# Hybrid encoder trunk on one core: first FFN's weight loads cut into halves and quarters, two adaLN sums moved to the stage's head, last FFN's adaLN loads issued ahead of its units

## The chip, the cores and the metric

The kernel runs on one core of one Trainium2 chip. The time is what the device takes for one execution, in microseconds (us); shown are the median of three runs and one further execution that the hardware profiler recorded. Differences here are a per cent or less, so every argument is about single stalls in the recorded execution.

## The reference

A trunk of two layers on a sequence of 512 tokens, width 1024, all in float32. Layer 0 mixes tokens with a gated short convolution, layer 1 with a Mamba-2 scan; each is followed by a SwiGLU feed-forward block (FFN) of width 2816. Every sub-layer is normed before and after, and shifted, scaled and gated by vectors that come from one conditioning vector `c`:

```python
mod = (jax.nn.silu(c) @ ada_w + ada_b).reshape(bsz, DEPTH, 2, 3, D_MODEL)
for i in range(DEPTH):
    shift, scale, gate = (mod[:, i, 0, k][:, None, :] for k in range(3))
    h = rmsnorm(x, norm_g[i, 0]) * (1.0 + scale) + shift
    y = short_conv_mixer(...) if i % N_MIXERS == 0 else ssd_mixer(...)
    x = x + gate * rmsnorm(y, norm_g[i, 1])
    shift, scale, gate = (mod[:, i, 1, k][:, None, :] for k in range(3))
    h = rmsnorm(x, norm_g[i, 2]) * (1.0 + scale) + shift
    y = swiglu_ffn(h, f_w_in[i], f_w_out[i])      # (silu(gate) * up) @ w_out
    x = x + gate * rmsnorm(y, norm_g[i, 3])
```

`silu(c) @ ada_w` is a vector times a 1024 x 12288 matrix: 48 MB of weights that are read once and used for almost no arithmetic. The kernel spreads these sums ("adaLN sums") over the whole program.

## The kernel before

**Arithmetic.** A float32 matrix product is made of three reduced-precision ones: each operand is split into a high part (a cast by ACT, lines 230 and 616) and a low part (the difference, by DVE, lines 231 and 617), and PE multiplies high by high, high by low and low by high. So every weight tile passes through one ACT and one DVE instruction after its load and before its matmuls.

**adaLN sums.** One sum (`ada_madd`, lines 125 and 127) multiplies 128 rows by 1024 columns of `ada_w` (a 512 KB load into a tile `ada_st`) by a column of `silu(c)` and adds it to an accumulator on DVE. Eight sums make one vector; then `ada_fold` (line 140) reduces the accumulator, `ada_fin` (line 147) finishes it with one small matmul, and four small additions write it. In the first FFN, `ada_steps` owns three `ada_st` buffers: as soon as a sum has read its buffer, `ada_load` (line 1004) issues the load for the sum three further on. `sums(n)` does the next n sums; 48 are done in this stage. In the last FFN, `gate_late` does eight sums for the very last gate vector, with two buffers that lie in a tile `raw`, which is not yet in use there.

**The first FFN** (it is the code around line 1345). At its head, PE finishes the last products of six column tiles that were begun before (`rest`), while DVE and ACT prepare other forms of the activations (`Values`). Then come six units (class `Units`), in which a 2 x 2 block product is done with seven products instead of eight; each unit fetches its weights in five loads (`fetch`, lines 602 to 608), and two further DMAs of GpSimd's queue (`add_`, line 1228) add weight blocks in place. Line 605 writes into the buffer that the last such addition has read, so it waits for that addition to land. After the units comes a loop over plain column tiles, k = 18 to 37. One tile is 24 matmuls of 128 x 512 (`in_chunk`). Per tile the loop also issues:

- every second tile, one load of 1 MB for the pair of tiles k + 4 and k + 5 (`load_pair_at`, through line 221, tile `wst`);
- at k = 18, 22 and 26 one load of 1 MB of the FFN's second weight matrix (`x_load`, line 1234, tile `w2x`);
- the splits of the weights of tile k + 2 (lines 230 and 231);
- two adaLN sums, with three at k = 24, and with each sum one load of 512 KB.

**The last FFN** has the same head and then 16 units. In unit u it calls `next(late, None)` behind `c12`, which is one step of `gate_late`: the first step issues the loads 0, 1 and, behind the first sum, 2; the eighth step does the last sum and the fold.

**Order.** In both FFNs the order on SP (which issues nearly all loads), ACT, DVE and GpSimd is the order of the code, and PE's is so throughout. An instruction that waits holds back all that stands behind it on its engine. On SP this means that a load that waits for a buffer holds back all later loads.

Of the kernel before, what the change touches and what calls it, by code (L numbers as in the profile page):

```python
# [8 lines left out]
F32 = mybir.dt.float32  # L9
F32R = mybir.dt.float32r  # L10
# [6 lines left out]
P = 128  # L17
T = 512
D = 1024
KD = D // P  # L20
DFF = 2816
# [17 lines left out]
def trunk_kernel(  # L39
# [175 lines left out]
    def load_w(srcs, nk=KD, k0=0, later=None):  # L215


        st = wst_p.tile([P, 8, 256], F32, tag="wst", name="wst")
        o = 0
        for m, c0, n in srcs:  # L220
            dma(st[:, :nk, o:o + n], m[k0 * P:(k0 + nk) * P, c0:c0 + n].rearrange("(k p) f -> p k f", p=P))
            o += n
        res = []
        for b in range(o // P):
            w = whl_p.tile([P, 2, 8, P], F32R, tag="whl", name="whl")
            sw = st[:, :nk, b * P:(b + 1) * P]
            if later is None:
                split_w(sw, w, nk)
            else:
                later.append((lambda sw=sw, w=w: act.copy(w[:, 0, :nk, :], sw),  # L230
                              lambda sw=sw, w=w: dve.tensor_tensor(w[:, 1, :nk, :], sw,  # L231
                                                                   w[:, 0, :nk, :].bitcast(F32), SUB)))
            res.append(w)
        return res
# [517 lines left out]
    with ExitStack() as ph:  # L752
# [477 lines left out]
        def w_rows(p, c, n=1):  # L1230
            return w2[2 * p * P:2 * (p + n) * P, c * T:(c + 1) * T].rearrange("(k p) f -> p k f", p=P)

        def x_load(u):
            dma(wx[u].rearrange("p i r f -> p (i r) f"), w_rows(2 * u, 0, 2))

        def y_load(p):
            wy[p] = hp.tile([P, 2, T], F32, tag=f"h{p}", name="w2y")
# [96 lines left out]
        with tc.manual_schedule(engines={PE_ENGINE, mybir.EngineType.SP, mybir.EngineType.Activation,  # L1334
# [11 lines left out]
                vs.value(j)  # L1346
            vs.first()
            vs.hi(0, va[:, :, lo_])
            rest(2)
            vs.value(4)  # L1350
            vs.value(5)
# [113 lines left out]
            splits = {k0 + i: op for i, op in enumerate(splits[5:])}  # L1465
            todo_w, todo_s = [], []

            def load_pair_at(k):
                got = []
                new = load_w([(f_w_in[0], (k - 2) // 2 % 2 * DFF + (4 + (k - 2) // 4 * 2) * P, 256)], later=got)  # L1470
                for i in range(2):
                    ws[k + i], splits[k + i] = new[i], got[i]

            for k in range(k0, last + 1):
                if k % 2 == 0 and k + 4 <= last:
                    load_pair_at(k + 4)
                if k in (k0, k0 + 4, k0 + 8):
                    x_load((k - k0) // 4)
                if k in (last - 2, last - 1):
                    xy_load(n_s - 2 + k - last + 2)  # L1480
                tiles[k] = in_chunk(ws[k], h)
                for step in todo:
                    next(step, None)
                q, j = divmod(k - 3, 4)
                if j < 2:
                    gate(4 + 2 * q + j, tiles[k - 1])
                else:
                    up(2 + 2 * q + j, tiles[k - 1])
                for op in splits.get(k + 2, ()):
                    op()  # L1490
                low_parts()
                sums(3 if k == k0 + 6 else 2)
                if k == 2 * NF - 12:
                    ggs.append(make_gg(1, gg_tile))
                if k == last - 1:
                    assert next(madds, 0) == 0 and not ada_sets and not quarters
                    sums_p.close()
                    ph.enter_context(tc.tile_pool(name="gap", bufs=1, side="right", reuse_waits="tile")).tile(
                        [P, 216], F32, tag="gap", name="gap")
                    ao_p.append(ph.enter_context(tc.tile_pool(name="aop", bufs=3, side="right", reuse_waits="tile")))  # L1500
                    ao_p[0].tile([P, 2, 2, 256], F32R, tag="ao", name="ao")
                    gotp = ph.enter_context(tc.tile_pool(name="gotp", bufs=1, side="right", reuse_waits="tile"))
                    c22 = gotp.tile([P, 2, T], F32, tag="c22", name="c22")
                if k >= last - 1:
                    w_prep(seq[k - last + 1])
                    a_prep(seq[k - last + 1])
# [563 lines left out]
    with ExitStack() as ph:  # L2070
# [137 lines left out]
        with tc.manual_schedule(engines={PE_ENGINE, mybir.EngineType.SP, mybir.EngineType.Activation,  # L2208
# [22 lines left out]
            def gate_late():  # L2231

                st = [raw[:, 18 + 2 * b:20 + 2 * b, :].rearrange("p a b -> p (a b)") for b in range(2)]
                acc = s1t[:, 7:11, :].rearrange("p a b -> p (a b)")
                part = s1t[:, 6, P:P + 32]

                def load(k):
                    if k < KD:
                        dma(st[k % 2], ada_w[k * P:(k + 1) * P, 88 * P:96 * P])

                load(0)
                load(1)
                for k in range(KD):
                    ada_madd(acc, st[k % 2], k)
                    load(k + 2)
                    if k == KD - 1:
                        ada_fold(acc, part)
                    yield
                yield from ada_fin(88 * P, part)
                yield from put_gates(3)  # L2250

# [39 lines left out]
            up(2, acc)  # L2291
            t_four(0)
            late = gate_late()
            for u in range(UN):
                v = u - 1
                last = u == UN - 1
                if u + 2 <= UN:
                    fetch(u + 2)
                elif last:
                    tail = []  # L2300
                    n12 = load_w([(w1, 21 * P, P), (w1, DFF + 20 * P, P)], later=tail)
                product(u, "P1")
                if u:
                    c12(v)
                    next(late, None)
                else:
                    t_four(1)
                    up(3, acc2)
                split_x(u + 1)
                if u:  # L2310
                    product(v, "P7")
                keep(u, "A", 0, LO)
                product(u, "P5")
                if u:
                    c22(v)
                    s13()
                product(u, "P2")
                keep(u, "C", 1, HI)
                if u:
                    product(v, "P4")  # L2320
                c11(u)
                split_z(u)
                if not last:
                    sum_y(u + 1)
                    sum_s(u + 1)
                product(u, "P6")
                if u:
                    c21(v)
                if last:
                    for op in tail[0]:  # L2330
                        op()
                    n3 = load_w([(w1, DFF + 21 * P, P)], later=tail)
                else:
                    split_y(u + 1)
                product(u, "P3")
                keep(u, "A", 0, HI)
                if not last:
                    split_s(u + 1)
# [184 lines left out]
```

## Time and profile before

| | us |
|---|---|
| median of three runs | 1345.19 (1344.96 to 1347.11) |
| the profiled execution, whole | 1347.34 |
| its span, first to last instruction | 1345.6 |
| PE busy in the span | 1314.5 |
| DVE busy | 1049.8 |
| ACT busy | 662.6 |

PE idles for 31 us in all. The rows that the next parts show are of these kinds. In a list of instructions by time, a row gives start and duration in us, engine, source line, operation, what it writes and reads, how many were merged, and in brackets how long the engine was idle ahead of it and whose end released it. In a table of stretches, the columns are the stretch, its length, then busy time of PE, PE's weight loads, DVE, ACT and GpSimd (POOL) with their number of instructions, then the granted PE clock as a share of full speed, the share of the time that the 16 DMA engines were busy, and GB/s. SPq is the queue of SP. "DMA a<-b" is a transfer in flight.

### The profile page before, as it was taken

The numbers are of one execution on the slowest core, as the hardware profiler recorded it, in microseconds if no ns is written. First come the engines' busy times: TensorE is split into PE (matmuls) and PEld (weight loads), VectorE is DVE, ScalarE is ACT, GpSimd is POOL, SyncE is SP. The second block draws the span as 40 slices with busy tenths as digits, with TensorE's granted clock in tenths as the row PEclk, the third lists the DMA queues.
The fourth block names the chain that finished last, engine by engine and source line by source line (L and its number), as shares of the span: only waits on it lengthen the run. The fifth ranks groups of instructions, "written<-read, shape, count | busy, mean of one in ns | idle before, by whom it ended". The sixth has DMA issues, their size and how long they took to land.

```text
span 1345.6 us, 19807 instructions
## 1 busy us (share of the span) xinstructions
PE 1314.5 (98%) x7653; PEld 1143.0 (85%) x7653; DVE 1049.8 (78%) x1627; ACT 662.6 (49%) x1084; POOL 99.5 (7%) x123
## 2 busy tenths in 40 slices
PE   8999999999999999999999999999999799999998
PEld 6788889998877788898888888888899799998886
DVE  5578667887877886768998988987678687776888
ACT  5333355443122565655555455564474354554665
POOL 0000000110000140000000000000002112100330
PEclk9999999999999999999999999999999899999999
DMA  9767742587888892415444334323334699768871
GB/s 311 235 205 242 236 153 60 152 209 233 291 311 278 231 177 71 121 33 162 139 118 133 104 100 131 121 79 120 131 87 110 189 248 236 196 165 285 186 140 63
DMA packets 209698, 228.53 MB, mean 170 GB/s; under 512 B 9396, under 2 KB 163908, under 8 KB 208580
## 3 DMA queue, kind: packets, MB, share of 16 engines
q1 hardware_dynamic: 191008, 187.88, 44.9%
q0 software_dynamic: 14448, 26.48, 11.4%
q10 hardware_dynamic: 4148, 12.90, 2.9%
q8 instruction: 60, 0.98, 0.3%
q14 instruction: 34, 0.28, 0.1%
HBM read 198.52 MB, written 2.24 MB: 149 GB/s over the span
## 4 chain that ended last, share of the span: by engine, by line
PE 82%; DMA 8%; DVE 5%; SPq 2%; ACT 2%; issue 2%; DVEq 0%; ACTq 0%; POOLq 0%
PE ip L285 10%; PE ip L287 10%; PE ip L286 10%; PE y L387 10%; PE sA L654 8%; DMA ada_st<-in_ada_w_dram 5%; PE cA L2205 4%; PE sC L654 4%; PE cA L1309 3%; PE li L285 2%; PE li L287 2%; PE li L286 2%; PE sB L654 2%; DVE ada_acc L127 2%; PE li L936 1%
## 5 line engine op out<-in xcount | busy, mean ns | idle before, releaser
L287 PE MATMUL ip<-h,whl 128*128 128x512 f32 x744 | 290.7, 391 | 5.6 <-DVE whl L231 5.6
L285 PE MATMUL ip<-h,whl 128*128 128x512 f32 x744 | 294.0, 395 | 1.8 <-ACT whl L230 1.6
L286 PE MATMUL ip<-h,whl 128*128 128x512 f32 x744 | 289.8, 389 | 0.0
L287 PEld LDWEIGHTS ip<-h,whl 128*128 128x128 f32 x744 | 139.7, 188 | 37.9 <-DVE whl L231 8.5
L285 PEld LDWEIGHTS ip<-h,whl 128*128 128x128 f32 x744 | 139.8, 188 | 31.5 <-ACT whl L230 1.8
L286 PEld LDWEIGHTS ip<-h,whl 128*128 128x128 f32 x744 | 139.8, 188 | 28.0
L231 DVE TENSOR_TENSOR whl<-wst,whl 128x1024 fp32r<-128x1024 f32 x86 | 104.4, 1219 | 31.3 <-ACT whl L230 31.3
L654 PE MATMUL sA<-tq,whl 128*128 128x256 f32 x792 | 106.0, 289 | 11.7 <-DVE g L681 9.8
L230 ACT CAST whl<-wst 128x1024 fp32r<-128x1024 f32 x86 | 89.2, 1042 | 48.6 <-DMA wst<-in_f_w_in_dram 46.4
L654 PEld LDWEIGHTS sA<-tq,whl 128*128 128x128 f32 x792 | 101.2, 197 | 13.2 <-DVE g L681 10.4
L127 DVE SCALAR_TENSOR_TENSOR ada_acc<-ada_st,csil,ada_acc 128x1024 f32<-128x1024 f32 x63 | 80.7, 1281 | 19.6 <-DMA ada_st<-in_ada_w_dram 19.1
L387 PE MATMUL y<-whlo,ys 128*128 128x512 f32 x384 | 89.4, 392 | 0.0
L387 PEld LDWEIGHTS y<-whlo,ys 128*128 128x128 f32 x384 | 71.7, 188 | 15.9 <-issue 0.6
L285 PE MATMUL li<-h,whl 128*128 128x256 f32 x288 | 83.2, 289 | 0.0
L287 PE MATMUL li<-h,whl 128*128 128x256 f32 x288 | 81.6, 283 | 0.0
L286 PE MATMUL li<-h,whl 128*128 128x256 f32 x288 | 81.5, 283 | 0.0
L617 DVE TENSOR_TENSOR whl<-wsu,whl 128x1024 fp32r<-128x1024 f32 x46 | 56.2, 1222 | 25.0 <-ACT whl L616 25.0
L1668 DVE SCALAR_TENSOR_TENSOR cu<-ip,cols,cu 128x511 f32<-128x511 f32 (+2 forms) x84 | 62.8, 748 | 3.9 <-ACT cu L1665 1.4
L2205 PE MATMUL cA<-whlo,ao 128*128 128x512 f32 x264 | 61.0, 390 | 0.4 <-DVE c L2436 0.2
L2205 PEld LDWEIGHTS cA<-whlo,ao 128*128 128x128 f32 x264 | 49.3, 188 | 11.5 <-ACT whlo L2170 1.2
L285 PEld LDWEIGHTS li<-h,whl 128*128 128x128 f32 x288 | 55.3, 192 | 0.0
L1228 POOL DMA_DIRECT2D sg<-sg x22 | 19.1, 870 | 488.5 <-DMA sg<-in_f_w_in_dram 287.9
(383 smaller groups left out, 2527.8 us busy)
## 6 DMA issues: line engine op xcount, KB each, us to landing
ada_st<-in_ada_w_dram SPq DMA_DIRECT2D x88, 512.0 KB, 6.0
wst<-in_f_w_in_dram SPq DMA_DIRECT2D x18, 1024.0 KB, 6.1
wst<-in_m_w_in_dram SPq DMA_DIRECT2D x14, 1024.0 KB, 5.3
wsu<-in_f_w_in_dram SPq DMA_DIRECT2D x24, 512.0 KB, 5.7
sg<-in_f_w_in_dram SPq DMA_DIRECT2D x44, 256.0 KB, 3.3
wsu<-in_f_w_in_dram SPq DMA_DIRECT2D x44, 256.0 KB, 3.9
wst<-in_m_w_in_dram SPq DMA_DIRECT2D x20, 512.0 KB, 4.8
wst<-in_a_w_in_dram SPq DMA_DIRECT2D x9, 1024.0 KB, 7.8
```

What stands on the lines that cost most here:

```text
L127: dve.scalar_tensor_tensor(acc, w, csil[:, k:k + 1], acc, MUL, ADD)
L230: later.append((lambda sw=sw, w=w: act.copy(w[:, 0, :nk, :], sw), lambda sw=sw, w=w: dve.tensor_tensor(w[:, 1, :nk, :], sw, w[:, 0, :nk, : ...
L231: lambda sw=sw, w=w: dve.tensor_tensor(w[:, 1, :nk, :], sw, w[:, 0, :nk, :].bitcast(F32), SUB)))
L285: pe.matmul(dst, w_at(w, 0, kk), a[:, 0, sl], start=start, stop=False)
L286: pe.matmul(dst, w_at(w, 0, kk), a[:, 1, sl], start=False, stop=False)
L287: pe.matmul(dst, w_at(w, 1, kk), a[:, 0, sl], start=False, stop=stop)
L387: pe.matmul(pst, a[:, al, tk], wt[:, wl, kk, :], start=k == 0 and i == 0, stop=k == K - 1 and i == 2, skip_group_check=bool(held))
L617: dve.tensor_tensor(dst[:, 1], src, dst[:, 0].bitcast(F32), SUB)
L654: pe.matmul(dst, w[:, wl, k0 + k, :], self.moving(q, k, al), skip_group_check=True, start=q in self.FIRST and k == 0 and i == 0, stop=k == ...
L1309: pe.matmul(bank[r, sub], a[:, al, q, tk], w[:, wl, q, :], start=first and k == 0, stop=False, skip_group_check=True)
L1668: dve.scalar_tensor_tensor(u[:, sft:], pst[:, :T - sft], w[3 - sft], u[:, sft:], MUL, ADD)
L2205: pe.matmul(bank[r][sub], a[:, al, q, tk], w[:, hl, q, :], start=first and k == 0, stop=last and k == 2, skip_group_check=True)
```

## The change

It has four edits.

1. In the loop of the first FFN the pair's 1 MB load becomes two loads of 512 KB (`load_pair_at(k, half)`): the first half at the even tile as before, the second at the odd tile after it. Each `x_load` of 1 MB becomes four of 256 KB, one per tile from k = 18 to 29.
2. At the head of the first FFN, `sums(2)` stands between two steps of the preparation on DVE. In return k = 24 has two sums, and k = 21 and k = 26 one each.
3. In the last FFN one step of `gate_late` is taken before the units; it issues loads 0 and 1 and nothing else.
4. There, `ada_fold` is a step of its own, a unit behind the eighth sum; what follows is a unit later too.

```diff
-        def x_load(u):
-            dma(wx[u].rearrange("p i r f -> p (i r) f"), w_rows(2 * u, 0, 2))
+        def x_load(u, i):
+            dma(wx[u].rearrange("p i r f -> p (i r) f")[:, i:i + 1, :], w_rows(2 * u, 0, 2)[:, i:i + 1, :])
...
             vs.first()
             vs.hi(0, va[:, :, lo_])
+            sums(2)
             rest(2)
             vs.value(4)
...
-            def load_pair_at(k):
-                got = []
-                new = load_w([(f_w_in[0], (k - 2) // 2 % 2 * DFF + (4 + (k - 2) // 4 * 2) * P, 256)], later=got)
-                for i in range(2):
-                    ws[k + i], splits[k + i] = new[i], got[i]
+            pair_st = {}
+
+            def load_pair_at(k, half):
+                if half == 0:
+                    st = pair_st[k] = wst_p.tile([P, 8, 256], F32, tag="wst", name="wst")
+                    for i in range(2):
+                        w = ws[k + i] = whl_p.tile([P, 2, 8, P], F32R, tag="whl", name="whl")
+                        src = st[:, :, i * P:(i + 1) * P]
+                        splits[k + i] = (lambda w=w, src=src: act.copy(w[:, 0], src),
+                                         lambda w=w, src=src: dve.tensor_tensor(w[:, 1], src,
+                                                                                w[:, 0].bitcast(F32), SUB))
+                c0 = (k - 2) // 2 % 2 * DFF + (4 + (k - 2) // 4 * 2) * P
+                dma(pair_st[k][:, 4 * half:4 * half + 4, :],
+                    f_w_in[0][half * T:(half + 1) * T, c0:c0 + 256].rearrange("(k p) f -> p k f", p=P))
 
             for k in range(k0, last + 1):
-                if k % 2 == 0 and k + 4 <= last:
-                    load_pair_at(k + 4)
-                if k in (k0, k0 + 4, k0 + 8):
-                    x_load((k - k0) // 4)
+                if k - k % 2 + 4 <= last:
+                    load_pair_at(k - k % 2 + 4, k % 2)
+                if k < k0 + 12:
+                    x_load(*divmod(k - k0, 4))
...
-                sums(3 if k == k0 + 6 else 2)
+                sums(1 if k in (k0 + 3, k0 + 8) else 2)
...
                 load(0)
                 load(1)
+                yield
                 for k in range(KD):
                     ada_madd(acc, st[k % 2], k)
                     load(k + 2)
-                    if k == KD - 1:
-                        ada_fold(acc, part)
                     yield
+                ada_fold(acc, part)
+                yield
                 yield from ada_fin(88 * P, part)
...
             late = gate_late()
+            next(late)
             for u in range(UN):
```

What this does to the engines' orders is shown at three places. The first is SP in the loop of the first FFN, from k = 18 on (`wst`: weights of column tiles, `w2x`: the FFN's second matrix, `ada_st`: rows of `ada_w`). Before:

```order
L221 DMA wst<-in_f_w_in_dram 128x8x256
L1234 DMA w2x<-in_f_w_out_dram 128x4x512
L1004 DMA ada_st<-in_ada_w_dram 128x1024 x4
L221 DMA wst<-in_f_w_in_dram 128x8x256
L1004 DMA ada_st<-in_ada_w_dram 128x1024 x4
L221 DMA wst<-in_f_w_in_dram 128x8x256
L1234 DMA w2x<-in_f_w_out_dram 128x4x512
L1004 DMA ada_st<-in_ada_w_dram 128x1024 x2
```

Now:

```order
L1481 DMA wst<-in_f_w_in_dram 128x4x256
L1234 DMA w2x<-in_f_w_out_dram 128x512
L1004 DMA ada_st<-in_ada_w_dram 128x1024 x2
L1481 DMA wst<-in_f_w_in_dram 128x4x256
L1234 DMA w2x<-in_f_w_out_dram 128x512
L1004 DMA ada_st<-in_ada_w_dram 128x1024 x2
L1481 DMA wst<-in_f_w_in_dram 128x4x256
L1234 DMA w2x<-in_f_w_out_dram 128x512
L1004 DMA ada_st<-in_ada_w_dram 128x1024 x2
```

Where 2 MB stood ahead of four adaLN loads, 0.75 MB now stand ahead of every two; the second half of a pair stands behind the two adaLN loads of the even tile.

The second place is SP at the units of the last FFN (`sg`, `wsu`: a unit's weights, `raw`: the adaLN rows). Before, from the fetch for unit 2 on:

```order
L602 DMA sg<-in_f_w_in_dram 128x4x128
L603 DMA sg<-in_f_w_in_dram 128x4x128
L605 DMA wsu<-in_f_w_in_dram 128x4x128
L606 DMA wsu<-in_f_w_in_dram 128x8x128
L608 DMA wsu<-in_f_w_in_dram 128x4x128
L602 DMA sg<-in_f_w_in_dram 128x4x128
L603 DMA sg<-in_f_w_in_dram 128x4x128
L605 DMA wsu<-in_f_w_in_dram 128x4x128
L606 DMA wsu<-in_f_w_in_dram 128x8x128
L608 DMA wsu<-in_f_w_in_dram 128x4x128
L2239 DMA raw<-in_ada_w_dram 128x1024 x3
```

Now, from the same place:

```order
L2249 DMA raw<-in_ada_w_dram 128x1024 x2
L602 DMA sg<-in_f_w_in_dram 128x4x128
L603 DMA sg<-in_f_w_in_dram 128x4x128
L605 DMA wsu<-in_f_w_in_dram 128x4x128
L606 DMA wsu<-in_f_w_in_dram 128x8x128
L608 DMA wsu<-in_f_w_in_dram 128x4x128
L602 DMA sg<-in_f_w_in_dram 128x4x128
L603 DMA sg<-in_f_w_in_dram 128x4x128
L605 DMA wsu<-in_f_w_in_dram 128x4x128
L606 DMA wsu<-in_f_w_in_dram 128x8x128
L608 DMA wsu<-in_f_w_in_dram 128x4x128
L2249 DMA raw<-in_ada_w_dram 128x1024
```

Two of the three adaLN loads have moved from behind the fetches for units 2 and 3 to ahead of both.

The third place is DVE at the eighth sum of the last FFN, in unit 8. Before:

```order
L672 TENSOR_TENSOR raw<-sC,raw 128x256
L674 TENSOR_TENSOR raw<-raw,g 128x512
L127 SCALAR_TENSOR_TENSOR s1t<-raw,csil,s1t 128x1024
L140 TENSOR_REDUCE s1t<-s1t 128x32
L617 TENSOR_TENSOR whl<-wsu,whl 128x1024
L681 SCALAR_TENSOR_TENSOR raw<-sA,raw 128x256
```

Now, from the eighth sum to the fold:

```order
L127 SCALAR_TENSOR_TENSOR s1t<-raw,csil,s1t 128x1024
L617 TENSOR_TENSOR whl<-wsu,whl 128x1024
L681 SCALAR_TENSOR_TENSOR raw<-sA,raw 128x256
L668 TENSOR_TENSOR g<-sB,g 128x256
L617 TENSOR_TENSOR whl<-wsu,whl 128x1024
L633 TENSOR_TENSOR sg<-sg,wsu 128x512
L637 TENSOR_TENSOR wsu<-sg,wsu 128x512
L689 TENSOR_TENSOR raw<-raw,g 128x512
L617 TENSOR_TENSOR whl<-sg,whl 128x1024
L617 TENSOR_TENSOR wss<-wsu,wss 128x512
L672 TENSOR_TENSOR g<-sC,g 128x256
L140 TENSOR_REDUCE s1t<-s1t 128x32
```

The fold (line 140) stood between the eighth sum and the split that line 681 stands behind; now it stands in unit 9, behind that unit's line 672.

## The prediction

> **What bounds the kernel now.** I read the page's engine shares and chain first, then stretches of 10 us over both FFNs, then the waits in the stretches where PE idles. The page:
>
> ```profile
> PE 1314.5 (98%) x7653; PEld 1143.0 (85%) x7653; DVE 1049.8 (78%) x1627; ACT 662.6 (49%) x1084; POOL 99.5 (7%) x123
> ...
> PE 82%; DMA 8%; DVE 5%; SPq 2%; ACT 2%; issue 2%; DVEq 0%; ACTq 0%; POOLq 0%
> ```
>
> PE bounds the kernel: nothing but its idle time can be won here, and the lower clock that follows some of it. The change touches two places where PE idles. The stretches of the first FFN's loop, with who PE and DVE waited for there:
>
> ```profile
> 370.00:380.00 10.00, 10.00 (x47) 8.29 (x46) 4.79 (x6) 2.60 (x3) 0.00 (x0) 1.00 1.03 380
> 380.00:410.00 30.00, 25.73 (x112) 20.10 (x111) 23.67 (x31) 4.14 (x5) 0.00 (x0) 1.00 0.83 281
> 410.00:450.00 40.00, 37.00 (x161) 29.57 (x160) 31.52 (x39) 12.64 (x17) 0.00 (x0) 1.00 0.73 244
> ...
> PE ip L287 <- DVE whl L231: 5.6, 6, 1.5
> ...
> DVE ada_acc L127 <- DMA ada_st<-in_ada_w_dram: 18.5, 10, 6.4
> ```
>
> PE idles 30 - 25.73 + 40 - 37.00 = 7.3 us there, at full clock, in pieces of at most 1.5. It waits for weight splits on DVE, and DVE in its turn loses 18.5 us to adaLN loads. When, is seen in the list by time, SP and DVE together:
>
> ```profile
> 344.00 1.11 SPq L1234 DMA_DIRECT2D w2x<-in_f_w_out_dram  x1
> 347.36 10.36 SPq L1004 DMA_DIRECT2D ada_st<-in_ada_w_dram  x4
> 356.07 1.28 DVE L127 SCALAR_TENSOR_TENSOR ada_acc<-ada_st,csil,ada_acc 128x1024 f32<-128x1024 f32 x1 [4.35 <-DMA ada_st<-in_ada_w_dram]
> 368.22 0.84 SPq L1234 DMA_DIRECT2D w2x<-in_f_w_out_dram  x1
> 381.28 1.28 DVE L127 SCALAR_TENSOR_TENSOR ada_acc<-ada_st,csil,ada_acc 128x1024 f32<-128x1024 f32 x1 [6.43 <-DMA ada_st<-in_ada_w_dram]
> 394.71 1.10 SPq L1234 DMA_DIRECT2D w2x<-in_f_w_out_dram  x1
> 406.09 1.28 DVE L127 SCALAR_TENSOR_TENSOR ada_acc<-ada_st,csil,ada_acc 128x1024 f32<-128x1024 f32 x1 [3.67 <-DMA ada_st<-in_ada_w_dram]
> ```
>
> Each of the three 1 MB loads of `w2x`, issued right behind a 1 MB load of `wst`, is followed some 12 us later by one long DVE wait: 4.35 + 6.43 + 3.67 = 14.5 of the 18.5 us. In the last FFN:
>
> ```profile
> 1048.83 7.82 SPq L2239 DMA_DIRECT2D raw<-in_ada_w_dram  x3
> 1055.55 0.75 DVE L125 TENSOR_SCALAR s1t<-raw,csil 128x1024 f32<-128x1024 f32 x1 [9.30 <-DMA raw<-in_ada_w_dram]
> 1057.82 4.39 PE L654 MATMUL sA<-tq,whl 128*128 128x256 f32 x24 [8.61 <-DVE g L681]
> 1083.82 2.88 PE sA L654 x24
> 1129.03 1.25 DVE L140 TRANSPOSE_TENSOR_REDUCE s1t<-s1t 128x32 f32<-128x1024 f32 x1
> 1131.77 4.65 PE L654 MATMUL sA<-tq,whl 128*128 128x256 f32 x24 [1.89 <-DVE raw L681]
> ```
>
> The adaLN loads are issued at 1048.83, when DVE already stands at the sum that needs them; it waits 9.30 us, and PE 8.61 behind it. At the fold DVE is late again, and PE idles 1.89. After both, 24 matmuls take 4.39 and 4.65 us where 2.88 is usual, because the granted clock drops.
>
> **The change part by part.** *Early loads, last FFN.* The loads 0 and 1 now follow the fetch for unit 1:
>
> ```profile
> 1027.40 0.58 SPq L608 DMA_DIRECT2D wsu<-in_f_w_in_dram  x1
> ```
>
> They are issued at about 1028, over 17 us before DVE reaches the sum (1055.55 - 9.30 = 1046.25). So the 9.30 us go, line 681 runs before PE asks for it, and 8.61 + (4.39 - 2.88) = **10.1 us** go. That is the upper end; the lower is 0, if the loads still came late.
>
> *Fold a unit later.* The eighth sum and the fold stand in two units, each with no more on DVE than the units before, which had no stall. 1.89 + (4.65 - 2.88) = **3.7 us** go; at worst the fold's own 1.25 is paid once in unit 9, so the gain is 2.4 to 3.7. I take 3.7, since DVE does only line 672 and no line 674 ahead of it there.
>
> [...]
>
> *What is late next, last FFN.* The long stall also gave the weight fetches time. Line 605 waits until GpSimd's addition into the preceding buffer has landed, and this circle is slower than a unit:
>
> ```profile
> 1043.46 2.88 PE sA L654 x24
> 1046.36 0.44 SPq L605 DMA_DIRECT2D wsu<-in_f_w_in_dram  x1
> 1064.73 0.45 SPq L605 DMA_DIRECT2D wsu<-in_f_w_in_dram  x1
> 1114.04 2.88 PE sA L654 x24
> 1120.75 0.37 SPq L605 DMA_DIRECT2D wsu<-in_f_w_in_dram  x1
> 1121.92 1.23 DVE L617 TENSOR_TENSOR whl<-wsu,whl 128x1024 fp32r<-128x1024 f32 x1 [1.58 <-ACT whl L616]
> 1128.83 0.37 SPq L605 DMA_DIRECT2D wsu<-in_f_w_in_dram  x1
> ...
> 275.50 0.37 SPq L605 DMA_DIRECT2D wsu<-in_f_w_in_dram  x1
> 298.45 0.37 SPq L605 DMA_DIRECT2D wsu<-in_f_w_in_dram  x1
> ```
>
> From 1064.73 to 1120.75 are five steps of 11.2 us, each with one adaLN load; without one, the step to 1128.83 takes 8.1. The first FFN, with such a load in every unit, shows 11.5 (22.95 / 2). A unit of PE takes (1114.04 - 1083.82) / 3 = 10.07. So the fetch loses 1.1 us per unit. In unit 7 it is issued 1120.75 - 1114.04 = 6.7 us after the unit's first matmul; the split behind it then already waits (1.58 us, through ACT). I take 6.6 as what PE bears. Before, the stall put the fetch back to a fresh start at 1064.73. Now it starts from 1046.36 - 1043.46 = 2.9 in unit 1 and makes six steps with adaLN loads: 2.9 + 6 x 1.13 = 9.7, so PE must give **3.1 us** back over units 4 to 8, in pieces under 1.5 us, which cost no clock. Bounds: 0 with steps of 10.5; with steps of 11.5, and a start 2 us later because the two early loads stand in the way of the addition for unit 1, 2.9 + 2 + 8.6 - 6.6 = 6.9.
>
> *Head of the first FFN.* Two sums, 0.75 + 1.28 us (the same operations as at 1055.55 and 356.07), now stand in front of the additions into `raw`:
>
> ```profile
> 181.55 7.38 SPq L1004 DMA_DIRECT2D ada_st<-in_ada_w_dram  x2
> 237.41 1.22 DVE L714 TENSOR_TENSOR tq<-va,tq 128x1024 fp32r<-128x1024 f32 x1 [2.83 <-ACT tq L709]
> ```
>
> Their data were issued by 189; DVE idles 2.83 us right there, waiting for ACT. So they cost **0**, with 0.8 us to spare; without that cover, 2.0 us of DVE in a stretch where PE did not wait. In return the loop has two sums and two 512 KB loads fewer by its ninth tile.
>
> *Loop of the first FFN.* The rows that price it:
>
> ```profile
> 325.05 1.43 PE sA L654 x12
> 343.59 1.22 DVE L231 TENSOR_TENSOR whl<-wst,whl 128x1024 fp32r<-128x1024 f32 x1
> 468.50 10.88 PE cB L1309 x48
> DMA to landing us min/median/max: 4.5/6.2/8.6
> L127 DVE SCALAR_TENSOR_TENSOR ada_acc<-ada_st,csil,ada_acc 128x1024 f32<-128x1024 f32 x35 | 44.9, 1282 | 18.9 <-DMA ada_st<-in_ada_w_dram 18.5
> L230 ACT CAST whl<-wst 128x1024 fp32r<-128x1024 f32 x86 | 89.2, 1042 | 48.6 <-DMA wst<-in_f_w_in_dram 46.4
> ...
> ada_st<-in_ada_w_dram SPq DMA_DIRECT2D x42, 512.0 KB, 6.1
> ```
>
> (The fourth is of the `ada_st` loads in the loop.) A column tile is 24 matmuls, 10.88 / 2 = 5.44 us. Per tile 0.5 + 0.25 + 1 MB must come, 1.835 MB / 5.44 us = 337 GB/s; from 370 to 380 the engines moved 380. So the average fits, and without the bursts the 14.5 us of DVE waits have no cause. But the second half of a pair is now issued behind the even tile's sums, a tile later than before, and needed at the next even tile. On DVE a pair of tiles then costs at least: issue 0.5, landing L, cast 1.04, split 1.22, two sums 2.56, half a fold and small things 0.7, together L + 6.0 against 10.88. PE loses L - 4.9 per pair, eight times, less the lead: the split at 343.59 ends at 344.8, and PE starts that tile at 325.05 + 1.43 + 4 x 5.44 = 348.2, 3.4 us later. L is between 4.5 and 6.2, the least and the median of equal loads among the bursts. I take 5.5, between the two, as the bursts are gone but two adaLN loads still stand ahead: 8 x 0.6 - 3.4 = 1.4 us of idle time stay, **5.9** of 7.3 go. At 4.9 or less all 7.3 go; at 6.2, 8 x 1.3 - 3.4 = 7.0 stay.
>
> **Sum.** 10.1 + 3.7 - 3.1 + 0 + 5.9 = 16.6 us. The profiled execution's span of 1345.6 becomes 1329.0; the 1.7 us around it (1347.34 whole) stay, 1330.7. It was 2.15 above the median of the runs shown, so on that scale 1345.19 - 16.6 = **1328.6**.
>
> **Rivals.** *Everything goes:* the fetch circle keeps up and the second halves are in time, 7.3 + 13.8 = 21.1, **1324.1**. For it: 8.1 us per step without an adaLN load. Against: 11.2 and 11.5 with one. *The loop stays as it is:* L is 6.2, the wait moves from the adaLN loads to the halves. 16.6 - 5.5 = 11.1, **1334.1**. For it: 337 GB/s is near what was ever moved. *The early loads are not early,* because `raw` is still held: the change does not do what it says. The 10.1 stay, the fetches keep their fresh start and 3.1 are not given back: 9.6, **1335.6**. Against it: `raw` is new memory in this stage, and SP went straight from 1027.40 to waiting for the next fetch.
>
> *Slower:* the second halves land late enough for PE to stall beyond 1.9 us, and each stall also costs clock. At L = 6.8 a pair costs 1.9 + 1.8 = 3.7, eight pairs 29.6 - 3.4 = 26.2, against 7.3 + 10.7 won: + 8.2, **1353.4**. It decides from L = 6.8 on. For it: the slowest load took 8.6. Against: that one stood behind 2 MB, and now 0.75 MB do. [...]
>
> **How the numbers follow.** Forecast 0.50, everything goes 0.16, loop as it is 0.20, not early 0.05, slower 0.09. The likeliest case's own range is 1324 to 1333 (5.9 + or - 1.5, 3.1 with its bounds). Taking in the first three rivals, with the circle at its worse bound beside the second (1334.1 + 3.8), gives **1322 to 1338**. A run of this kernel tells 0.2%, 2.7 us, from no change. All cases but the last are faster by more: faster 0.89, same 0.02 (the border of the last), slower 0.09.
>
> **What would show it.** Right: no DVE wait for `raw` in the last FFN's unit 1 and full clock there; no PE wait at the fold; line 605 drifting past 6.6 us after a unit's start by unit 4, with PE waits under 1.5 us in units 4 to 8; in the loop, DVE waits for `ada_st` under 5 us in sum, and short waits of the even tiles' casts for `wst`. Wrong: PE idle over 3 us between 330 and 450, a clock under 1.00 there, a PE wait at the first FFN's head, or steps of line 605 near 10 us.

## The result, and the profile after

| | us |
|---|---|
| after, median of four runs | 1334.04 (1332.90 to 1338.59) |
| before, beside it on the same chip | 1345.08 (1344.84 to 1347.11) |
| ratio | 0.9921, 95% interval 0.9895 to 0.9947 |
| profiled execution of after, whole | 1334.83 (before 1347.34) |
| its span | 1333.0 (before 1345.6) |

The change makes the kernel 0.8% faster; the forecast of 1328.6 was 5.4 us too good. That is inside its range of 1322 to 1338, but outside the 1324 to 1333 that it gave its likeliest case. The profiled execution of before lies 2.3 us above its median and that of after 0.8, so the traces show a larger gain (12.6) than the medians (11.0). From the page of after, PE's line and the chain of waits:

```profile
PE 1314.0 (99%) x7653; PEld 1140.6 (86%) x7653; DVE 1049.6 (79%) x1627; ACT 662.4 (50%) x1084; POOL 99.5 (7%) x123
...
PE 74%; DMA 11%; DVE 8%; ACT 3%; issue 2%; SPq 2%; ACTq 0%; DVEq 0%; POOLq 0%
```

The table of stretches: the first FFN's loop in the same three as before, and then the last FFN (1040 to 1060 holds unit 1, 1115 to 1135 the fold):

```profile
370.00:380.00 10.00, 10.00 (x46) 8.30 (x46) 6.90 (x13) 2.25 (x4) 0.00 (x0) 1.00 0.85 275
380.00:410.00 30.00, 29.92 (x133) 24.43 (x133) 23.41 (x28) 6.21 (x8) 0.00 (x0) 1.00 0.93 312
410.00:450.00 40.00, 37.30 (x158) 28.38 (x157) 30.67 (x38) 11.31 (x16) 0.00 (x0) 1.00 0.71 231
...
1040.00:1060.00 20.00, 19.72 (x163) 19.41 (x162) 16.84 (x24) 10.65 (x19) 3.23 (x4) 1.00 0.93 236
1060.00:1115.00 55.00, 53.44 (x441) 52.83 (x440) 43.57 (x58) 27.78 (x48) 8.41 (x11) 1.00 0.90 236
1115.00:1135.00 20.00, 19.25 (x159) 18.90 (x158) 17.29 (x23) 10.56 (x19) 3.91 (x5) 1.00 0.97 239
```

From 380 to 410 us PE hardly idles any more, but from 410 to 450 it still loses 2.70 us (3.00 before). In the last FFN the clock is full throughout. At the sum of unit 1 and at the fold, where PE had waited 8.61 and 1.89 us and the next 24 matmuls had taken 4.39 and 4.65, it now reads

```profile
1046.48 3.13 PE L654 MATMUL sA<-tq,whl 128*128 128x256 f32 x24 [0.28 <-DVE g L681]
...
1120.71 3.14 PE L654 MATMUL sA<-tq,whl 128*128 128x256 f32 x24 [0.75 <-DVE raw L681]
```

Small losses are left in units 6 to 8. Line 605 in the units 1 and 7, six steps apart:

```profile
1043.96 0.37 SPq L605 DMA_DIRECT2D wsu<-in_f_w_in_dram  x1
...
1110.93 0.37 SPq L605 DMA_DIRECT2D wsu<-in_f_w_in_dram  x1
```

What took over in the first FFN's loop is the first of these rows of DVE's waits:

```profile
DVE whl L1478 <- ACT whl L1477: 23.4, 10, 3.6
...
DVE ada_acc L127 <- DMA ada_st<-in_ada_w_dram: 2.7, 4, 0.9
```

and, from the group of the loads of the halves there, their number and their times from issue to landing:

```profile
L1481 SPq DMA_DIRECT2D wst<-in_f_w_in_dram x16: 385/427/577, 343.7 to 431.6; - x16
...
DMA to landing us min/median/max: 5.4/6.6/7.5
```

The waits for adaLN loads fell from 18.5 to 2.7 us. In their place DVE waits 23.4 us for ACT's casts. In seven of the ten waits, 18.5 us, the cast had waited for a second half; in the other three, of 1.6 us each, it stood on ACT behind line 1201, which had waited for DVE. The halves land 6.6 us after their issue in the median.

Where the time went is seen best by comparing the start of the same matmul in both traces, since PE takes the products in the same order. After minus before, in us:

```
first FFN: at 304 us  0.0 | 364 -0.5 | 415 -7.4 | 441 -4.9 | 488 -3.7
last FFN:  at 986 us -3.0 | 1049 -12.6 | 1118 -9.9 | 1127 -12.8 | end -12.6
```

So the loop wins 7 us and gives more than half of it back, the early loads win 9.6, the fetch circle takes 2.5 to 2.7, and the fold wins 2.9. Between 964 and 986 us, 0.7 is lost where nothing was changed. A kernel that differs from the one before only at the last FFN's fold lost 1.9 there, and another, which is the changed kernel up to that place, nothing: it varies from execution to execution, and its cause was not sought. The loop's gain is steadier: from 304 to 488 us the two other kernels with this loop (the first FFN's part alone, eight loads ahead) gain 4.3 and 3.3 us, this one 3.7.

### The profile page after: what moved, and what is told of

It reads as the page before. It is cut to its first block, busy times and chain, and to the rows that moved or that the text cites. A ratio compares the mean times of both kernels' runs of the same rounds, so it can differ in the third digit from the quotient of the medians.

```text
span 1333.0 us, 19834 instructions
## 1 busy us (share of the span) xinstructions
PE 1314.0 (99%) x7653; PEld 1140.6 (86%) x7653; DVE 1049.6 (79%) x1627; ACT 662.4 (50%) x1084; POOL 99.5 (7%) x123
## 3 DMA queue, kind: packets, MB, share of 16 engines
q0 software_dynamic: 14448, 26.48, 11.4%
## 4 chain that ended last, share of the span: by engine, by line
PE 74%; DMA 11%; DVE 8%; ACT 3%; issue 2%; SPq 2%; ACTq 0%; DVEq 0%; POOLq 0%
PE ip L285 10%; PE ip L287 10%; PE ip L286 10%; PE y L387 8%; PE sA L654 5%; PE cA L2215 4%; DMA wsu<-wsu 4%; DMA wst<-in_f_w_in_dram 4%; PE cA L1309 3%; PE sC L654 2%; PE li L285 2%; PE li L287 2%; PE li L286 2%; DVE ada_acc L127 2%; PE li L936 1%
## 5 line engine op out<-in xcount | busy, mean ns | idle before, releaser
L231 DVE TENSOR_TENSOR whl<-wst,whl 128x1024 fp32r<-128x1024 f32 x70 | 84.8, 1219 | 24.7 <-ACT whl L230 24.7
L654 PEld LDWEIGHTS sA<-tq,whl 128*128 128x128 f32 x792 | 98.3, 192 | 5.7 <-DVE g L681 2.5
L230 ACT CAST whl<-wst 128x1024 fp32r<-128x1024 f32 x70 | 72.7, 1041 | 11.1 <-DMA wst<-in_f_w_in_dram 9.0
L616 ACT CAST whl<-wsu 128x1024 fp32r<-128x1024 f32 x46 | 48.1, 1045 | 18.7 <-PE sB L654 7.8
```

Of the source, the lines that this page charges most:

```text
L231: lambda sw=sw, w=w: dve.tensor_tensor(w[:, 1, :nk, :], sw, w[:, 0, :nk, :].bitcast(F32), SUB)))
L616: act.copy(dst[:, 0], src)
L654: pe.matmul(dst, w[:, wl, k0 + k, :], self.moving(q, k, al), skip_group_check=True, start=q in self.FIRST and k == 0 and i == 0, stop=k == ...
```

## The experiments

Ratios are to the kernel before on the same chip, with their 95% intervals; the matmuls that PE starts between 370 and 470 us are from the table of stretches (one takes 10.88 / 48 = 0.227 us there; 447 is the count in the kernels in which PE never idles).

| kernel | median us | ratio | matmuls, 370 to 470 |
|---|---|---|---|
| before | 1345.1 to 1347.6 | 1 | 405 |
| after | 1334.04 | 0.9921 (0.9895 to 0.9947) | 418 |
| first FFN's part alone | 1345.40 | 0.9985 (0.9970 to 1.0000) | 423 |
| last FFN's part alone | 1337.39 | 0.9937 (0.9918 to 0.9955) | 402 |
| after, pair load whole | 1328.32 | 0.9867 (0.9840 to 0.9893) | 447 |
| after, halves by column tile | 1328.97 | 0.9872 (0.9847 to 0.9897) | 447 |
| after, `w2x` loads whole | 1337.33 | 0.9934 (0.9915 to 0.9954) | 411 |
| pair whole, no sums at the head | 1331.55 | 0.9888 (0.9868 to 0.9909) | 428 |
| fold alone | 1345.67 | 0.9991 (0.9979 to 1.0003) | 405 |
| after, eight loads ahead | 1340.26 | 0.9952 (0.9938 to 0.9966) | 415 |
| halves by column tile, spaced loads | 1327.72 | 0.9859 (0.9837 to 0.9881) | 447 |
| pair whole, spaced loads | 1326.73 | 0.9854 (0.9833 to 0.9874) | 447 |

### The two FFNs apart

The kernel before with edits 1 and 2 alone:

> The kernel before with the first FFN's part of the change alone (halves, quarters, the two sums at the stage's head). Theory (the terms of the prediction add up, the first FFN's being smaller than forecast): the changed kernel's trace is 3.6 us ahead of the one before when the first FFN's products are done, so this kernel should gain 3 to 4 us, about 1341.5, and the last FFN should look as before: 8.61 us of PE waiting for the adaLN loads in unit 1, 1.89 at the fold. Rival (the lead is lost in between, as the 0.7 us lost at the last boundary hints): no more than 1 us faster. Rival (the forecast of 5.9 was right and the last FFN took some of it back): 5 to 6 us faster.

The kernel before with edits 3 and 4 alone:

> The kernel before with the last FFN's part alone (early loads, and the fold a unit later). Theory: the changed kernel's trace wins 9.6 us at the early loads, loses 2.5 to the fetch circle and wins 2.9 at the fold, so 9 to 10 us faster, about 1335.5, with line 605 drifting past 6.6 us behind a unit's first matmul by unit 4 to 6 as in the changed kernel. Rival (the last FFN gains only because the first FFN's part shifts something): under 6 us. Rival (the prediction's own terms, 10.1 + 3.7 - 3.1): 10.7 us.

By the ratios the first FFN's part is worth 2.0 us and the last FFN's 8.5; both together gave 10.6. Within their intervals they add up. The first kernel's 2.0 us, with an interval from 0 to 4.0, lie between its theory (3 to 4) and its first rival (no more than 1) and decide for neither. The second kernel's 9.6 us by the medians are what its theory said; by the ratio they are 8.5. The first part's trace gains 4.3 us from 304 to 488 us, but nearly all of that is gone at the end, 0.9 of it at the boundary, the rest at the last FFN's stalls, which this kernel still has. The row of its long stall:

```profile
1055.13 5.49 PE L654 MATMUL sA<-tq,whl 128*128 128x256 f32 x24 [8.74 <-DVE g L681]
```

The wait is that of before (8.61), but the 24 matmuls behind it take 5.49 us, not 4.39. In the second kernel's trace the early loads win 9.6, the circle takes 1.4 back, and the fold wins 2.9.

### Which cut of the loads helps

The changed kernel with the pair's load whole again:

```diff
...
-                if k - k % 2 + 4 <= last:
-                    load_pair_at(k - k % 2 + 4, k % 2)
+                if k % 2 == 0 and k + 4 <= last:
+                    load_pair_at(k + 4)
```

> The changed kernel with the 1 MB load of a pair whole again at the even tile; the loads of w2x stay in quarters. Theory (the quarters took the bursts away, and the halves by rows only brought lateness): as with halves by column tile, PE idles under 1 us from 390 to 470 us, DVE's waits for the adaLN loads stay under 9 us, about 4 us faster than the changed kernel, near 1330. Rival (1 MB at once is itself a burst, behind which the two adaLN loads of the tile come late): DVE waits over 12 us for them in the loop, PE idles 2 to 5 us, as the changed kernel or up to 2 us slower.

The changed kernel with the loads of `w2x` whole again:

```diff
...
-                if k < k0 + 12:
-                    x_load(*divmod(k - k0, 4))
+                if k in (k0, k0 + 4, k0 + 8):
+                    x_load((k - k0) // 4)
```

> The changed kernel with the three 1 MB loads of w2x whole again (at the first, fifth and ninth tile of the loop); the pair's load stays in halves by rows. Theory (each w2x load was the burst that cost DVE 3.7 to 6.4 us): three long DVE waits are back, 2.5 to 5 us each, and PE idles 5 to 8 us from 380 to 470 us, 2 to 4 us slower than the changed kernel, about 1337. Rival (the bursts came from the two 1 MB loads together, and half a pair beside a whole w2x is no burst): waits for the adaLN loads under 5 us in sum, same time as the changed kernel within 1 us.

The changed kernel with halves by columns, each of which serves one column tile:

```diff
-                dma(pair_st[k][:, 4 * half:4 * half + 4, :],
-                    f_w_in[0][half * T:(half + 1) * T, c0:c0 + 256].rearrange("(k p) f -> p k f", p=P))
+                c0 += half * P
+                dma(pair_st[k][:, :, half * P:(half + 1) * P],
+                    f_w_in[0][:, c0:c0 + P].rearrange("(k p) f -> p k f", p=P))
```

> The changed kernel, with the pair's 1 MB load in halves by column tile (128 columns of all rows) in place of halves by rows; each half is then due two tiles after its issue, where the second half by rows was due one tile after. Theory (the first FFN's idle time that is left comes from the second half's lateness): the 23.4 us in which DVE's splits wait for ACT's casts fall under 5, PE's 2.8 us of idle time from 390 to 450 us and the 0.7 at 462 fall under 1 in sum, 2.5 to 3.5 us faster than the changed kernel, about 1331. Rival (the transfers are at their limit: 337 GB/s asked for, 380 the most seen): the wait moves to the adaLN loads, over 10 us on DVE, and PE's idle time stays at 2.5 to 3.5. Rival (512-byte pieces of rows arrive more slowly than 1024-byte ones): landing over 7.5 us in the median, PE's idle time grows.

With the pair whole, the stretch of the loop and the first products reads

```profile
370.00:470.00 100.00, 100.00 (x447) 82.69 (x446) 80.52 (x107) 37.46 (x55) 10.39 (x12) 1.00 0.87 267
```

DVE's longest sum of waits in the loop, and the landing of the 1 MB loads there:

```profile
DVE ada_acc L127 <- DMA ada_st<-in_ada_w_dram: 10.6, 9, 2.4
```

```profile
DMA to landing us min/median/max: 7.1/7.5/7.9
```

PE does not idle at all. The adaLN loads do come late again, 10.6 us in sum (over the 9 of the expectation), but in nine pieces of at most 2.4, which PE's lead bears; the rival's mechanism is there, and its price is not. With halves by columns, the casts' waits on DVE and the landing of the halves:

```profile
DVE whl L1478 <- ACT whl L1477: 7.6, 7, 1.6
```

```profile
DMA to landing us min/median/max: 5.4/6.5/7.9
```

These halves are issued at the same places, are of the same size and land as late (6.5 against 6.6 us); only what needs them is different, a tile later. The casts' waits fall from 23.4 to 7.6 us (under 5 was expected) and PE's idle time goes: 447 matmuls again. The 7.6 us that are left are in seven pieces of at most 1.6, and in none of them had the cast waited for a load. So the loss was neither bandwidth nor the cutting, but that a pair's *second half by rows* holds up the casts of both tiles. With `w2x` whole and halves by rows, the longest wait for an adaLN load, in the list by time:

```profile
355.24 1.28 DVE L127 SCALAR_TENSOR_TENSOR ada_acc<-ada_st,csil,ada_acc 128x1024 f32<-128x1024 f32 x1 [3.22 <-DMA ada_st<-in_ada_w_dram]
```

The waits for adaLN loads are 7.3 us in sum, against 18.5 before and 2.7 in the changed kernel: half a pair beside a whole `w2x` is a smaller burst than two whole loads, as the rival said, but no small one. Of the three long waits that the theory forecast, this is the only one over 2.5 us (the next are 2.00 and 1.60), and PE idles 4.7 us, not 5 to 8. The median is what the theory said, but the ratio's interval overlaps that of the changed kernel. The ratio is close to that of the last FFN's part alone: with `w2x` whole, edits 1 and 2 bring nothing that the time shows. The quarters carry the gain of edit 1: the kernel of the next part that has them, the pair whole and no sums at the head, differs from the last FFN's part alone by nothing else, and its ratio is 0.0049 lower, 6.6 us, with intervals that do not overlap. The halves by rows cost 0.0054 of the time, 7 us by the medians' ratios and 5.5 by the profiled executions (1334.83 against 1329.36).

### The sums at the head

Against the kernel with the pair's load whole:

```diff
             vs.hi(0, va[:, :, lo_])
-            sums(2)
             rest(2)
...
-                sums(1 if k in (k0 + 3, k0 + 8) else 2)
+                sums(3 if k == k0 + 6 else 2)
```

> The kernel with whole pair loads and quarters of w2x (and the last FFN's part), now without the two sums at the stage's head: they are back in the loop, three in its seventh tile and two in every other. Theory (the quarters alone took the bursts away; the head's sums cost nothing and bring next to nothing): PE idles under 1.5 us from 370 to 470 us, within 1.5 us of the kernel with the head's sums, near 1329. Rival (the loop needs its two sums and two 512 KB loads fewer): the DVE waits for the adaLN loads go over 14 us again and PE idles 3 to 6 us there, 3 to 5 us slower than with them.


 In the changed kernel the head's sums cost nothing, as forecast (0.0 us at 304). But the loop needs what they take out of it. PE's longest stall without them:

```profile
415.69 0.50 PE L285 MATMUL ip<-h,whl 128*128 128x512 f32 x1 [1.56 <-ACT whl L230]
416.03 0.40 PE L286 MATMUL ip<-h,whl 128*128 128x512 f32 x1
416.95 0.66 PE L287 MATMUL ip<-h,whl 128*128 128x512 f32 x1 [0.52 <-DVE whl L231]
```

Nineteen matmuls fewer, 4.3 us; by the ratios 2.8, with intervals that overlap. The DVE waits for adaLN loads stay at 12.3 us, under the rival's 14, and the loss is one stall with the lower clock behind it, so neither text had it right. In these two executions the sums at the head are worth 4 us in the loop; by time alone their gain is not clear of noise.

### The fold

The kernel before with edit 4 alone:

> The kernel before, with the fold of the last FFN's adaLN sums one unit later than the eighth sum, and nothing else. Theory (the 1.89 us stall and the lower clock after it both go): no PE wait at the fold, 24 matmuls in 2.88 us throughout units 8 and 9, 2.9 to 3.7 us faster, about 1342. Rival (the stall only moves to the unit in which the fold now stands): a PE wait of 1 to 2 us one unit later, under 1 us faster. Rival (the clock falls there for another reason): PE does not wait, but the granted clock is under 0.95 in the ten us after, 1.9 us faster.

```profile
1131.91 1.60 PE L654 MATMUL sB<-h,whl 128*128 128x256 f32 x12
1134.26 3.14 PE L654 MATMUL sA<-tq,whl 128*128 128x256 f32 x24 [0.75 <-DVE raw L681]
```

In the list of PE by time, the stall of 1.89 us becomes one of 0.75, where the expectation had none, and the clock stays full. The matmuls' starts gain 2.6 us there. The time shows it only as 0.9991, between 2.8 us faster and 0.4 slower, so by time alone this run is inconclusive. The 0.75 us are the fetch circle's: line 605 is late (7.2 us behind its unit's first matmul in unit 7), and DVE had waited for the split of that unit's weights (1.95 us, through ACT) before. The next part bears this out: where the circle keeps up, PE does not wait at the fold.

### The fetch circle

The changed kernel with all eight adaLN loads behind the first weight fetch:

```diff
...
-                load(0)
-                load(1)
+                for k in range(KD):
+                    load(k)
                 yield
                 for k in range(KD):
-                    ada_madd(acc, st[k % 2], k)
-                    load(k + 2)
+                    ada_madd(acc, st[k], k)
                     yield
...
+            late = gate_late()
+            next(late)
             vs = Values(h, tq, va, vb)
...
```

> The changed kernel, with all eight adaLN loads of the last FFN issued behind its first weight fetch, into rows of raw that no unit has written yet, so that no unit issues one. Theory (the fetch circle is slow because an adaLN load stands in the way of each addition): steps of line 605 at or under a unit's 10.07 us, no drift, the 2.3 us of PE idle time from 1090 to 1130 us go under 0.5, 2 to 2.5 us faster than the changed kernel, about 1331.5. Rival (the circle is slower than a unit by itself): steps stay at 11 us and the idle time stays. Rival (eight loads in a row hold SP or the queues up, so the fetch for unit 1 comes late): a new PE wait between 1020 and 1060, same time or slower.

SP's list by time, with GpSimd's addition for unit 1 and PE's stall between:

```profile
1022.62 3.85 SPq L2248 DMA_DIRECT2D raw<-in_ada_w_dram  x8
...
1038.22 0.90 POOL L1228 DMA_DIRECT2D sg<-sg  x1 [22.87 <-DMA sg<-in_f_w_in_dram]
...
1041.73 1.98 PE L654 MATMUL sA<-tq,whl 128*128 128x256 f32 x12 [3.93 <-ACT g L664]
...
1062.07 0.44 SPq L605 DMA_DIRECT2D wsu<-in_f_w_in_dram  x1
...
1112.53 0.44 SPq L605 DMA_DIRECT2D wsu<-in_f_w_in_dram  x1
```

and the stretch behind it:

```profile
1060.00:1130.00 70.00, 70.00 (x586) 70.00 (x585) 60.48 (x81) 36.02 (x62) 12.09 (x14) 1.00 0.84 209
```

Both the theory and the third text come true. From 1062.07 to 1112.53 are five steps of 10.09 us, a unit's own time, and from 1060 on PE never idles: without an adaLN load the circle keeps up. But SP could issue the loads only from 1022.62 on, 37 us behind the fetch, presumably since the memory of `raw` was in use until the last matmuls `li` of the stage's head. The weights for unit 1 were issued behind these 4 MB, from 1026.70 on: GpSimd's addition waits for them until 1038.22, PE waits 3.93 and 1.76 us, and with the clock that follows (0.89 from 1030 to 1060 us) it loses more than was won. Spaced loads, with four buffers (shown against the changed kernel):

```diff
...
-                load(0)
-                load(1)
+                for k in range(3):
+                    load(k)
                 yield
                 for k in range(KD):
-                    ada_madd(acc, st[k % 2], k)
-                    load(k + 2)
+                    ada_madd(acc, st[k % 4], k)
+                    if k in (0, 1, 3, 4, 5):
+                        load(k + 3 if k < 2 else k + 2)
                     yield
```

> The kernel with halves by column tile, and in the last FFN four buffers for the adaLN loads: three loads in front of the units, then one each in units 1, 2, 4, 5 and 6, so that the fetch circle gets back about 2 us in unit 3. Theory (a circle step costs 11.2 us with such a load and 8.1 or more without, and PE bears 6.6 us of lateness): line 605 stays under 6.6 us behind a unit's first matmul, PE's 3.4 us of waits from 1060 to 1120 fall under 1, 2 to 2.5 us faster than with halves by column tile alone, about 1326.5. Rival (three loads ahead are already a burst that makes the addition for unit 1 late, as eight were): a PE wait over 1 us between 1025 and 1045, no gain or slower.

> The kernel with whole pair loads and quarters of w2x, with the adaLN loads of the last FFN as in the kernel with halves by column tile and spaced loads (three ahead, then units 1, 2, 4, 5, 6). Theory (both parts add up): no PE wait over 0.7 us in either FFN, PE idles under 1 us from 370 to 470 and under 1 from 1030 to 1130, 20 to 22 us faster than the kernel before, a ratio of 0.984 to 0.986. Rival (the last FFN's gain of spacing was chance): waits of 2 us or more from 1060 to 1120 as in the changed kernel, a ratio of 0.987.

Both kernels have spaced loads, the first with halves by columns, the second with whole pair loads. In the first, line 605 around the unit without a load, and PE's only wait from 1060 to 1130 us:

```profile
1048.95 0.37 SPq L605 DMA_DIRECT2D wsu<-in_f_w_in_dram  x1
...
1060.32 0.37 SPq L605 DMA_DIRECT2D wsu<-in_f_w_in_dram  x1
...
1068.95 0.37 SPq L605 DMA_DIRECT2D wsu<-in_f_w_in_dram  x1
```

```profile
PE sA L654 <- DVE raw L681: 0.4, 1, 0.4
```

The step without a load takes 8.6 us, the one ahead of it 11.4, and 0.4 us of waits are left, at the fold. Three loads ahead are no burst that hurts. Against the same kernel with two buffers, 4 us are won in the profiled executions and 1.8 by the ratios, within their intervals and under the 2 to 2.5 of the expectation. With whole pair loads the waits from 1030 to 1130 fall from 2.7 to 1.3 us (under 1 was expected), and the one at the fold is 0.75 (0.7 was). The rival that spacing gains by chance is not ruled out by this: the kernel without sums at the head, which does not space its loads, waits only 1.0 us there. The two ratios are each 0.0013 below those with two buffers, and all four intervals overlap. The last kernel has the lowest ratio of all: 0.9854, 19.7 us below the kernel before, with an interval wholly below that of the changed kernel.

## Why the prediction was right, and where it was off

Of the 16.6 us that were forecast, the profiled execution shows 12.6, the medians 11.0 and the ratio 10.6. By the terms, from the profiled execution:

- **Early loads, 10.1 us.** Right: 9.6. The sum at unit 1 no longer waits, PE waits 0.28 us there and the clock stays full.
- **Fold, 3.7.** Right in mechanism, 2.9 measured (2.6 alone): a wait of 0.75 us stays, which the prediction had said would not, because DVE is late by the fetch circle then, not by the fold. It is 0.4 and 0.75 with spaced loads, and nothing where no unit issues a load.
- **Circle, -3.1.** Right in mechanism: -2.5 to -2.7, with steps of 11.2 us ((1110.93 - 1043.96) / 6). Line 605 passed 6.6 us behind a unit's first matmul in unit 5 (6.8), not by unit 4 (5.6). The experiment without loads in the units shows that these loads make it slow. That the size is so near is in part luck, since five other kernels with the same last FFN paid 0.4 (no sums at the head), 1.4 (last FFN's part alone), 2.1 (`w2x` whole), 3.0 (pair whole) and 3.3 us (halves by columns).
- **Head, 0.** Right.
- **Loop, 5.9.** Mis-sized: 3.2 by the matmuls' starts from 364 to 488 us, and this is the term that failed. The first step is L, the time to landing, taken as 5.5 us; it was 6.6, above the 6.2 at which the rival "the loop stays as it is" began. With it the formula leaves 8 x 1.7 - 3.4 = 10.2 us, more than there was to win, so the rest of the pair's circle was shorter than the 6.0 us assumed. Of the second halves the first was issued at 349.23 and the last, seven pairs on, at 431.61, 11.77 us apart on average (six steps of 10.7 to 11.9 and one of 14.0), which leaves 5.2 for that rest. Against PE's 10.88 this is 0.89 us per pair, not 0.6, and eight pairs less the lead of 3.4 make 3.7. What stayed in fact is seen beside the kernel with the pair whole, which gains 9.6 us over the same stretch: 6.4. The 3.5 us of idle time from 370 to 470 understate it, and that they are near 3.7 is chance. So the formula has the right cause but covers little more than half of its price; where the rest arises was not traced.
- **The ceiling of 7.3.** It was too low. PE started 405 matmuls where 447 fit, so 42 x 0.227 = 9.5 us were to be had, and the kernels without the late halves took them. Idle time in the table of stretches understates short stalls; the last section shows by how much.
- **The rivals.** "Everything goes" is what whole pair loads give in the loop. "The loop stays as it is" has the measured time almost exactly, 1334.1 against 1334.04, and its mechanism was there: the wait moved from the adaLN loads to the halves, with L above 6.2. The exact number is luck, for that rival wins only 0.4 us in the loop, where the trace shows 3.2. Of the slower case, the mechanism (the second halves come late) was there too, but at about 0.8 us per pair (6.4 / 8), and no stall passed 0.7 us. It was to decide from L = 6.8 on, 0.2 above what was measured.

The prediction priced edit 1 as one thing. It was two with opposite signs: the quarters, with the two sums moved to the head, win what the loop had to give, and the halves by rows take about 6 us of it back.

A 1 MB load landed 7.5 us after its issue (pair whole) and a 512 KB one 6.6 (in halves), so in these two kernels most of the delay did not go with size. Cutting cost nothing that the times show where each piece had its own reader (halves by columns, 0.9872 against 0.9867).

## What to carry to other kernels

Cut a large load only along the line on which its readers are cut: a half that every reader needs is just a later load (418 matmuls from 370 to 470 us with halves by rows, 447 by columns). Here the bursts on SP's queue made the 512 KB loads late (DVE waited 18.5 us for them before, 10.6 with the quarters and whole pair loads), so spread what has slack (the quarters); the rest need not be cut. Loads that were added to a circle with little slack did better spaced, with a turn to recover (a step of 8.6 us behind one of 11.4; ratio 0.9859 against 0.9872 with two buffers), than moved ahead in one block (0.9952 against 0.9921). That spacing also beats one load per turn, the traces suggest and the times do not show.

## What the runs showed of the hardware

**A short stall cost more than its idle time.** In the changed kernel:

```profile
427.34 0.40 PE L286 MATMUL ip<-h,whl 128*128 128x512 f32 x1
428.27 0.51 PE L287 MATMUL ip<-h,whl 128*128 128x512 f32 x1 [0.53 <-DVE whl L1478]
428.61 0.39 PE L285 MATMUL ip<-h,whl 128*128 128x512 f32 x1
```

Matmuls follow each other every 0.227 us there but last 0.39, so a wait of 0.16 us is not even seen as idle. Here the starts are 0.93 and 0.34 apart: 0.81 us lost with 0.53 shown. Ten such stalls would lose almost 3 us that is not shown, an estimate from this one (10 x 0.28). Counting matmuls in a stretch is the better measure.

**The clock fell behind one stall of 1.89 us, and behind two shorter ones.** The single stall at the fold of before, 1.89 us, brought the granted clock to 0.83 in the ten us from 1130, and 1.56 and 0.52 us of idle time within 2.8 us brought it to 0.86 in the ten us from 410 (the kernel without the head's sums), while a single stall of 0.75 left it at 1.00 from 1130 to 1140 (fold alone). In the loop of the kernel before, 1.13 and 0.53 us within 2.4 left it at 1.00 too (420 to 430), as did a single 1.49 (380 to 390). With a longest stall of 2.9 us in the loop (fold alone) it is 0.98 from 370 to 470, where before has 1.00. Where the border lies, these runs do not settle. After almost the same stall of 8.6 to 8.7 us the next 24 matmuls took 4.39 us in one execution and 5.49 in another. From 1050 to 1060 us the granted clock is 0.69 in the first (before) and 0.54 in the second (first FFN's part alone), and in the ten us after that 0.96 and 0.95. In before it is 0.50 from 1053.88 to 1060.71 us, 6.83 us, and behind the stall at the fold from 1132.39 to 1135.80, 3.41 us. What sets these lengths the runs do not show.

```profile
410.00:420.00 10.00, 7.92 (x30) 6.04 (x29) 7.40 (x8) 3.49 (x5) 0.00 (x0) 0.86 0.84 241
```
